# The last batch of a matrix-trace kernel: other load groups, and four rows instead of two on TensorE

## The chip, the cores and the metric

The kernel runs on one core of one Trainium2 chip. The metric is the device time of a run in microseconds (us). The span of the profile is 1.7 to 1.8 us shorter than the time of the same run.

The verdict "faster" or "slower" is given at 2%, which is 14.2 us here.

## The reference

```python
B, N = 8, 2176
prod = np.matmul(a, b)                                           # a, b: [8, 2176, 2176] float32
traces = np.diagonal(prod, axis1=1, axis2=2).sum(axis=-1)        # eight numbers
```

A trace needs no product: it is the sum over i and k of `a[i, k] * b[k, i]`. So the kernel reads both inputs once (303 MB), transposes A on TensorE, and multiplies it with B element by element.

## The kernel before

"Row" means a row block here: 128 rows of B, so a batch has 17 of them, 0 to 16. The loads turn float32 into bfloat16 on the way and are issued from GpSimd. In each batch A is loaded first. TensorE transposes it into PSUM, and ScalarE and VectorE copy it into the tile `at`. Then B is loaded, and VectorE multiplies `at` with B's rows and sums, one instruction for each load group:

```python
def multiply_reduce(x, y, acc, out=None):          # one VectorE instruction, sum into acc
    nc.vector.tensor_tensor_reduce(out=x if out is None else out, in0=x, in1=y, scale=1.0,
                                   scalar=0.0, op0=MUL, op1=ADD, accum_out=acc)
```

In the last batch nothing follows that could hide the work on B. So this batch has smaller load groups, and gives some rows to TensorE. There a row is 17 matmuls of 128 by 128, all added up in one PSUM tile; the diagonal of that tile holds the sums wanted:

```python
    fine = [4, 4, 2, 2, 2, 2, 1]                   # rows in each load of the last batch's B
    PE_ROWS = (13, 15)                             # rows that TensorE takes
    LAST_PIECES = [(0, 2), (2, 3), (3, 5)]         # row 16 is loaded in three pieces
    ...
                (group,), _ = fetch(shared[:, used:used + m, :], b[bi], start, m, 1)
                used += m
                b_t = group[2]
                mine = [s for s in range(m) if v0 + s not in PE_ROWS]
                on_dve(v0 + mine[0], b_t[:, mine[0]:mine[-1] + 1, :])
                for s in range(m):
                    if s not in mine:
                        multiply_on_pe(at, b_t[:, s, :], v0 + s, 0, len(a_groups))
    ...                                            # row 16: TensorE and VectorE share each piece
    for n, (x, y) in enumerate(pe_work):
        nc.tensor.matmul(trace_ps, x, y, start=(n == 0), stop=(n == len(pe_work) - 1))
    ...                                            # VectorE: its share of row 16's pieces, then
    multiply_reduce(tiles[f32], trace_ps, late_acc[:, cols:cols + 1], out=tiles["diagonal"])
    ...                                            # sum over partitions (TensorE, VectorE), store
```

I call the last `multiply_reduce` "the diagonal". It needs TensorE's last matmul, and in program order it follows all of VectorE's other work. About 2.8 us of sums and store come after it.

## Time and profile before

| | kernel before |
|---|---|
| median of six runs | 710.47 us (710.38 to 710.72) |
| span of the profile | 708.7 us |
| HBM read over the span | 428 GB/s |
| busiest compute engine | VectorE, 57% |
| last piece of B landed | 704.30 us |
| VectorE done, diagonal starts | 705.93 us |
| TensorE's last matmul ends | 705.66 us |

The stream of loads fills the span. The tail behind it decides, and it begins with three events that lie within 1.6 us of each other. The groups of VectorE's instructions in the last 37 us of the kernel before say how its work is divided (line, engine, operation, tiles, shapes, count | busy us, mean ns | idle before):

```profile
L133 DVE CUSTOM_DVE_ANT_1 at<-at,shared 128x8704 bf16<-128x8704 bf16 x2 | 18.4, 9223 | 0.5 <-ACT at L128 0.5
L133 DVE CUSTOM_DVE_ANT_1 at<-at,shared 128x4352 bf16<-128x4352 bf16 x2 | 9.3, 4685 | 0.0
L133 DVE CUSTOM_DVE_ANT_1 at<-at,shared 128x2176 bf16<-128x2176 bf16 x2 | 4.8, 2419 | 0.0
```

Six instructions, 32.5 us, with no waiting but 0.5 us at the start: VectorE is behind the loads throughout.

### The profile page before, as it was taken

The numbers are of one execution on the slowest core, as the hardware profiler recorded it, in microseconds if no ns is written. First come the engines' busy times: TensorE is split into PE (matmuls) and PEld (weight loads), VectorE is DVE, ScalarE is ACT, GpSimd is POOL, SyncE is SP. The second block draws the span as 40 slices with busy tenths as digits, with TensorE's granted clock in tenths as the row PEclk, the third lists the DMA queues.
The fourth block names the chain that finished last, engine by engine and source line by source line (L and its number), as shares of the span: only waits on it lengthen the run. The fifth ranks groups of instructions, "written<-read, shape, count | busy, mean of one in ns | idle before, by whom it ended". The sixth has DMA issues, their size and how long they took to land.

```text
span 708.7 us, 3160 instructions
## 1 busy us (share of the span) xinstructions
PE 193.3 (27%) x1271; PEld 179.6 (25%) x1271; DVE 403.7 (57%) x204; ACT 197.2 (28%) x211; POOL 36.0 (5%) x63
## 2 busy tenths in 40 slices
PE   1542006420054100551006600056000670006703
PEld 0542005420054100550006500056000560005602
DVE  0223995138942389423893348933489335883398
ACT  2344005430064200652006510066000670006700
POOL 1000000000010000000001000000000000000100
PEclk9977556765577655776557765577655775557755
DMA  9999999999999999999999999999999999999997
GB/s 220 220 219 214 210 221 220 218 209 214 224 219 214 214 218 221 216 212 216 220 218 216 214 217 220 212 217 218 217 216 215 216 220 218 214 214 217 220 211 145
DMA packets 11681, 152.28 MB, mean 215 GB/s; under 512 B 914, under 2 KB 1170, under 8 KB 3090
## 3 DMA queue, kind: packets, MB, share of 16 engines
q0 software_dynamic: 11520, 150.97, 100.2%
q1 hardware_dynamic: 146, 1.11, 0.5%
q8 instruction: 10, 0.16, 0.1%
q14 instruction: 5, 0.04, 0.0%
HBM read 303.04 MB, written 0.00 MB: 428 GB/s over the span
## 4 chain that ended last, share of the span: by engine, by line
DMA 53%; DVE 27%; another core or an unknown queue 8%; issue 7%; PE 2%; ACT 1%; POOL 0%; DVEq 0%; POOLq 0%
DMA t<-in_b_dram 41%; DVE at L133 27%; DMA t<-in_a_dram 13%; PE ps L167 2%; ACT at L128 1%; POOL t L82 0%; DVE acc L133 0%; PE ps L188 0%; POOL identity masks.py:199 0%; DVE late L133 0%; DVE at L126 0%; DVEq L133 0%; POOL identity masks.py:197 0%; PE total L322 0%
## 5 line engine op out<-in xcount | busy, mean ns | idle before, releaser
L128 ACT COPY at<-ps 128x1024 bf16<-128x1024 bf16 x208 | 194.8, 1045 | 471.6 <-PE ps L167 471.4
L133 DVE CUSTOM_DVE_ANT_1 at<-at,t 128x8704 bf16<-128x8704 bf16 (+1 forms) x35 | 273.6, 7863 | 80.8 <-DMA t<-in_b_dram 80.8
L167 PE MATMUL ps<-identity,t 128*128 128x128 f32 x1088 | 179.3, 332 | 479.2 <-DMA t<-in_a_dram 468.5
L167 PEld LDWEIGHTS ps<-identity,t 128*128 128x128 f32 x1088 | 167.3, 212 | 488.1 <-issue 460.8
L126 DVE COPY at<-ps 128x1024 bf16<-128x1024 bf16 (+2 forms) x104 | 94.1, 907 | 215.4 <-PE ps L167 197.7
L82 POOL DMA_DIRECT2D t<-in_a_dram x23 | 15.4, 669 | 343.2 <-DVE acc L133 199.6
L133 DVE CUSTOM_DVE_ANT_1 at<-at,shared 128x8704 bf16<-128x8704 bf16 (+2 forms) x6 | 32.3, 5442 | 0.5 <-ACT at L128 0.5
L82 POOL DMA_DIRECT2D t<-in_b_dram x23 | 14.8, 646 | 238.8 <-PE ps L188 119.5
L188 PE MATMUL ps<-identity,t 128*128 128x128 bf16 x136 | 14.2, 219 | 5.0 <-DVE at L126 4.6
L188 PEld LDWEIGHTS <-t 128*128 128x128 bf16 x136 | 11.0, 100 | 8.4 <-issue 8.3
L307 PEld LDWEIGHTS <-at 128*128 128x128 bf16 x40 | 4.6, 123 | 28.9 <-issue 28.8
L307 PE MATMUL trace_ps<-shared,at 128*128 128x128 bf16 x32 | 4.0, 293 | 28.4 <-DMA shared<-in_b_dram 28.4
L82 POOL DMA_DIRECT2D shared<-in_b_dram x6 | 3.2, 534 | 55.1 <-PE ps L188 35.8
L101 DVE CAST t<-words 128x1088 bf16<-128x1088 f32 x1 | 0.7, 727 | 5.0 <-DMA words<-in_a_dram 5.0
L133 DVE DVE_READ_ACCUMULATOR2_ANT acc<- 128x1 f32 x35 | 2.9, 83 | 0.0
L100 ACT CAST t<-words 128x1088 bf16<-128x1088 f32 x1 | 1.1, 1099 | 3.8 <-DMA words<-in_a_dram 3.8
L292 POOL DMA_DIRECT2D b_t<-in_b_dram x3 | 1.6, 559 | 0.0
L100 ACT ACT_TABLE_LOAD x1 | 1.3, 1283 | 0.7 <-PEq L346 0.7
L133 DVE CUSTOM_DVE_ANT_1 at<-at,b_t 128x256 bf16<-128x256 bf16 (+1 forms) x3 | 1.4, 507 | 0.0
L265 DVE TENSOR_REDUCE sums<-acc 128x1 f32<-128x5 f32 x7 | 1.1, 157 | 0.2
L307 PE MATMUL trace_ps<-b_t,at 128*128 128x128 bf16 x8 | 1.1, 296 | 0.0
L133 DVE DVE_READ_ACCUMULATOR2_ANT late<- 128x1 f32 x10 | 0.8, 82 | 0.0
(18 smaller groups left out, 4.2 us busy)
## 6 DMA issues: line engine op xcount, KB each, us to landing
t<-in_a_dram POOLq DMA_DIRECT2D x16, 4352.0 KB, 45.5
t<-in_b_dram POOLq DMA_DIRECT2D x14, 4352.0 KB, 51.9
shared<-in_b_dram POOLq DMA_DIRECT2D x2, 2176.0 KB, 42.7
shared<-in_b_dram POOLq DMA_DIRECT2D x4, 1088.0 KB, 34.1
t<-in_a_dram POOLq DMA_DIRECT2D x7, 544.0 KB, 47.4
t<-in_b_dram POOLq DMA_DIRECT2D x6, 544.0 KB, 54.9
words<-in_a_dram SPq DMA_DIRECT2D x1, 1088.0 KB, 5.1
t<-in_b_dram POOLq DMA_DIRECT2D x1, 340.0 KB, 53.7
```

Source lines behind the costliest of these rows:

```text
L82: issued = nc.gpsimd.dma_start(out=part[lo:hi], in_=rows[lo:hi])
L100: nc.scalar.copy(out=t[:, 0, :half], in_=plain[:, :half])
L101: nc.vector.tensor_copy(out=t[:, 0, half:], in_=plain[:, half:])
L126: last_copy = nc.vector.tensor_copy(out=dst, in_=src)
L128: nc.scalar.copy(out=dst, in_=src)
L133: nc.vector.tensor_tensor_reduce(out=x if out is None else out, in0=x, in1=y, scale=1.0, scalar=0.0, op0=MUL, op1=ADD, accum_out=acc,)
L167: nc.tensor.transpose(ps[:, n * m + r, :], words[:, r, c0:c0 + step * (P - 1) + 1:step], tiles[f32],)
L188: last_transpose = nc.tensor.transpose(ps16[:, n, r, :], a_t[:, r, c0:c0 + P], tiles[bf16],)
L265: nc.vector.reduce_sum(out=tiles["sums"][:, bi:bi + 1], in_=acc[:, :cols], axis=mybir.AxisListType.X)
L292: loaded.append(nc.gpsimd.dma_start(out=row[:, lo:hi], in_=b[bi, start:start + P, lo:hi]))
L307: nc.tensor.matmul(trace_ps, x, y, start=(n == 0), stop=(n == len(pe_work) - 1),)
```

## The change

The intent is to take VectorE out of the tail. TensorE, idle most of that time, gets rows 11 and 12 too, and rows 14 and 15 are loaded separately, so that VectorE can have row 14 as soon as it is there.

```diff
-    fine = [4, 4, 2, 2, 2, 2, 1]
+    fine = [4, 4, 4, 2, 1, 1, 1]
-    PE_ROWS = (13, 15)
+    PE_ROWS = (11, 12, 13, 15)
...
-                on_dve(v0 + mine[0], b_t[:, mine[0]:mine[-1] + 1, :])
+                if mine:
+                    on_dve(v0 + mine[0], b_t[:, mine[0]:mine[-1] + 1, :])
```

## The prediction

> **What bounds the kernel now.** I read the page first, then the chain of waits from 590 us on, then the timeline of the last 40 us, then the issues of GpSimd, and last the packets and completion increments of the DMA queue in the trace. The page says that the span is a stream of loads:
>
> ```profile
> span 708.7 us, 3160 instructions
> ...
> DMA  9999999999999999999999999999999999999997
> GB/s 220 220 219 214 210 221 220 218 209 214 224 219 214 214 218 221 216 212 216 220 218 216 214 217 220 212 217 218 217 216 215 216 220 218 214 214 217 220 211 145
> ...
> HBM read 303.04 MB, written 0.00 MB: 428 GB/s over the span
> ```
>
> The DMA engines are at 90% or more in 39 of 40 slices; only the last slice (17.7 us) drops to 7 tenths and 145 GB/s. No compute engine is above 57%. So a change to compute can win only what lies after the last byte, plus stalls of the stream, of which there are none to see. The change touches the last batch alone, so the stage to look at is the last 40 us. The chain of waits there:
>
> ```profile
> 672.42 8.54 DVE at L133
> ...
> 704.35 0.28 issue
> 704.63 0.08 DVE late L133
> 704.71 0.60 DVE at L133
> 705.31 0.01 DVE late L133
> 705.33 0.34 DVE at L133
> ...
> 705.93 0.08 DVE late L133
> 706.01 0.20 DVE diagonal L133
> ```
>
> From 672.42 to 706.21 VectorE is named at nearly every step: it starts when the transposed A is complete, and no gap follows. The "issue" pieces are the inside of long VectorE instructions. The timeline shows the tail of both engines (start, duration, engine, line, instruction):
>
> ```profile
> 690.71 4.68 DVE L133 CUSTOM_DVE_ANT_1 at<-at,shared 128x4352 bf16<-128x4352 bf16 x1
> ...
> 699.94 2.42 DVE L133 CUSTOM_DVE_ANT_1 at<-at,shared 128x2176 bf16<-128x2176 bf16 x1
> 702.28 2.01 PE L307 MATMUL trace_ps<-shared,at 128*128 128x128 bf16 x16 [3.59 <-DMA shared<-in_b_dram]
> ...
> 704.33 1.11 PE L307 MATMUL trace_ps<-b_t,at 128*128 128x128 bf16 x8
> 704.63 0.69 DVE L133 CUSTOM_DVE_ANT_1 at<-at,b_t 128x512 bf16<-128x512 bf16 x1
> ...
> 705.26 0.40 PE L307 MATMUL trace_ps<-at,b_t 128*128 128x128 bf16 x1
> 705.93 0.28 DVE L133 CUSTOM_DVE_ANT_0 diagonal<-identity,trace_ps 128x128 bf16<-128x128 f32 x1
> ```
>
> Two things are to be seen. VectorE is behind: it begins the first of row 16's pieces at 704.63. And TensorE, which waited 3.59 us for rows 14-15 and then ran to 705.66 (705.26 + 0.40), is behind VectorE's end by only 0.27 us (705.93 - 705.66). The completion increments in the trace (sixteen for each load; the last counts) give the landings: rows 8-9 at 686.13, 10-11 at 691.24, 12-13 at 696.42, 14-15 at 702.24, the three pieces of row 16 at 702.89, 703.50 and 704.30. So three things end within 1.6 us of each other: the stream (704.30), TensorE (705.66), VectorE (705.93). After that come the diagonal, the two last sums and the store, 2.81 us (708.74 - 705.93), which the change leaves alone.
>
> **What the Trainium skill says.** (1) "DMA: Bandwidth & Descriptors", section Bandwidth, measures 425 GB/s for a 16 MB load by a single core and derives a ceiling of 435.2 GB/s. The trace agrees: 428 GB/s over the whole span, so the stream has no slack to be won. (2) The same page, "Why a DMA increments its semaphore by 16 and not by 1": only the full 16 means that all data landed, so a load is as late as its slowest engine. The trace agrees: rows 14-15 have fifteen increments by 701.59 and the last at 702.24; a 16,384-byte instruction packet at 700.2 fell among its packets. (3) "VectorE: DVE Perf Modes", the section on the TRN2 errata, gives (N+151)/0.96 ns for an fp32 tensor_tensor add; the page has no row for this custom multiply-and-reduce, but it obeys that formula: 2176 elements give 2424 ns (trace 2419), 4352 give 4691 (4685), 8704 give 9224 (9223). (4) "TensorE: Matmul & The Clock Gate", Part 1: the array runs at half clock until about one window of 3413 ns has been busy. In the trace the grant is 0.50 from 673.99 to the end; it rose to 1.0 elsewhere after windows that I work out as 85% busy or more, and not after windows of up to 76% (a rough count from matmul starts).
>
> **The change, part by part.** *VectorE's work.* Before, rows 0-12 and 14 are its own: fourteen rows in six instructions, 672.42 to 704.63, 32.21 us. Afterwards it has rows 0-3, 4-7, 8-10 and 14: twelve rows in four. The first two take to 690.71 as before. Three rows have 6528 elements: (6528+151)/0.96 = 6.96 us, an estimate by the formula above; row 14 costs 2.42. Sum 18.29 + 6.96 + 2.42 = 27.67, so 4.5 us less. *Where that goes.* Rows 8-11 are one load now and land when 10-11 did, 691.2 to 691.3, so the third instruction starts 0.6 us later and ends at about 698.25. Row 14 has its own load and lands halfway between 696.42 and 702.0, near 699.2; VectorE waits about 1 us and ends it at 701.65. Then it follows row 16's pieces: 702.95 + 0.69 = 703.64; + 0.42 = 704.06; the last lands at 704.30, starts about 704.36 and ends at 704.78. VectorE would be done 1.15 us earlier than the 705.93 of before.
>
> *TensorE's work.* Two more rows, 17 matmuls each. One row costs 2.05 us (702.28 to 704.33). Row 11 runs 691.3 to 693.4, in idle time. Rows 12 and 13 run 696.46 to 700.6, before row 15 is there. So none of the two added rows delays row 15. Row 15 ends with the last byte of the same 2.2 MB (rows 14 and 15) as before and lands at 701.6 if the instruction packet falls elsewhere, 702.24 if it does not. Row 15 and row 16's nine matmuls took 3.38 us (702.28 to 705.66); so TensorE ends between 705.03 and 705.66. It cannot end earlier than about 705.0 anyway: the last piece lands at 704.30, and then three matmuls of its own follow (two at about 0.12 us pitch, and the last one's 0.40).
>
> *The end.* The diagonal then waits for TensorE, no longer for VectorE, and starts about 0.1 us after it (estimate, the hand-over of a semaphore): 705.1 to 705.75, against 705.93. That is 0.2 to 0.8 us won, and I take 0.5.
>
> *Transposes.* Rows 14 and 15 leave the paired fp32 form for single bf16: per group of four A rows, four fp32 transposes fewer and eight bf16 more. At full clock the trace has them 0.11 us and 0.055 us apart, so 0.44 against 0.44 us: nothing. The copies stay 9 for each such group, with the same size; ScalarE sits in a row from 664.04 to 672.42 and sets VectorE's start, so that start stays at 672.4, within 0.3 us. VectorE's later wait swallows such a shift.
>
> *The stream.* Nine loads before and nine after, in the same three buffers, let go by the same instructions. Packets of 17408, 8704 and 4352 bytes take 1302, 662 and 342 ns (medians). Rows 8-11 as one load: 8 packets for each engine, 10.42 us, against 16 x 662 = 10.59; rows 14 and 15 apart: 16 x 342 = 5.47 against 8 x 662 = 5.30. Minus 0.17 and plus 0.17: nothing.
>
> Sum: 710.49 - 0.5 = **710.0 us**.
>
> **The rivals.** *The whole VectorE saving arrives* (4.5 us, 706.0). For it: the chain of waits is VectorE throughout. Against it: the last byte lands at 704.30 and VectorE's end was 705.93, so no compute change can win more than 1.6 us. I give this nothing. *TensorE takes VectorE's place with no gain*: if row 15 lands at 702.24 again, or later because single-row packets end less evenly over the engines, the gain shrinks to 0.2 us or nothing, 710.3 to 710.5. For it: the 0.27 us between the two engines. *The stream gets longer*: another mean rate of small packets at the end, where the three pieces of row 16 already have packets of 1024 to 2048 bytes, or an issue that comes later because a transposition ends later. Queued loads stand 25 us ahead (rows 12-13 issued at 670.68, landed at 696.42), which speaks against the second. It would make 710.7 to 711. *The clock comes up*: rows 12 and 13 fill the window from 697.88 to 701.29 to about 77%, on the edge of what raised the grant elsewhere. Row 15 would then be quick, and the end would be set by the last landing: 709.6 to 709.8.
>
> **Range and chances.** Most weight lies between the second rival and the fourth, 709.6 to 710.5. The three runs of before differ by 0.34 us, which I add around it: 709.2 to 710.8. Two per cent are 14.2 us; there is nothing in these parts that moves a tenth of that in either direction. So within 2%: 0.98, and 0.01 on each side.
>
> **What would show each step right or wrong.** Right: VectorE has idle time before row 14's instruction, released by the load of row 14, and again before row 16's pieces; the 3-row instruction lasts about 6.95 us; the diagonal is released by TensorE rather than following VectorE; the last piece lands at 704.3 within 0.3; VectorE starts at 672.4. Wrong: VectorE without gaps to the end; the last landing beyond 704.8; row 15's matmuls starting later than 702.4; a grant of 1.0 after 701 (then the gain is nearer 0.8). A time above 711 would mean that the stream, not the tail, was hurt, and below 709 that it got shorter, which I see no reason for.

## The result, and the profile after

The changed kernel took 709.68 us (median of six runs, 709.64 to 710.19), the kernel before 710.47: 0.79 us less. Ratios are computed as the mean time of one kernel's runs over that of the other's of the same rounds, so they are not quite the ratio of the medians. Here the ratio is 0.999, with an interval from 0.9977 to 1.0003. The slowest of the six runs lies below the fastest of the other six.

The page of the changed kernel has the same stream:

```profile
span 707.9 us, 3257 instructions
...
DMA  9999999999999999999999999999999999999997
...
HBM read 303.04 MB, written 0.00 MB: 428 GB/s over the span
```

What differs is the end of the chain of waits (start, us, what):

```profile
671.22 30.32 DMA shared<-in_b_dram
701.54 0.04 issue
701.58 3.39 PE trace_ps L308 x26
...
705.12 0.29 DVE diagonal L133
```

Where VectorE stood from 672 us on, the chain now has one load (row 15, landed at 701.54) and then TensorE's 26 matmuls for rows 15 and 16. The timeline of the same stretch shows VectorE waiting, which it did not do there before:

```profile
691.32 6.96 DVE L133 CUSTOM_DVE_ANT_1 at<-at,shared 128x6528 bf16<-128x6528 bf16 x1 [1.10 <-DMA shared<-in_b_dram]
...
699.05 2.42 DVE L133 CUSTOM_DVE_ANT_1 at<-at,shared 128x2176 bf16<-128x2176 bf16 x1 [0.77 <-DMA shared<-in_b_dram]
...
701.58 2.01 PE L308 MATMUL trace_ps<-shared,at 128*128 128x128 bf16 x16 [0.91 <-DMA shared<-in_b_dram]
702.82 0.69 DVE L133 CUSTOM_DVE_ANT_1 at<-at,b_t 128x512 bf16<-128x512 bf16 x1 [1.34 <-DMA b_t<-in_b_dram]
...
704.26 0.43 DVE L133 CUSTOM_DVE_ANT_1 at<-at,b_t 128x256 bf16<-128x256 bf16 x1 [0.36 <-DMA b_t<-in_b_dram]
704.56 0.40 PE L308 MATMUL trace_ps<-at,b_t 128*128 128x128 bf16 x1
705.12 0.29 DVE L133 CUSTOM_DVE_ANT_0 diagonal<-identity,trace_ps 128x128 bf16<-128x128 f32 x1 [0.42 <-PE trace_ps L308]
```

VectorE waits for a load before four of its last five multiplications, in the square brackets. It ends row 16 at 704.69, and the diagonal waits 0.42 us more for TensorE. TensorE starts row 15 at 701.58, not 702.28 as before, and ends 0.70 us earlier, at 704.96.

So the 0.81 us (705.93 to 705.12) have two parts. The last piece landed 0.06 us earlier (704.24 against 704.30). And the diagonal starts 0.88 us after that landing, no longer 1.63. The second part, 0.75 us, is what the experiments are about. There is something odd in it: row 15 is the end of the same bytes as before, and yet it was complete 0.70 us earlier (702.24 before, 701.54 after). A 16,384-byte packet of instructions passed at 700.2 in the kernel before; in the changed kernel the last such packet passed at 673.0. So there are two candidates: the work that was moved away from VectorE, and a packet that happened to move.

### The profile page after: what moved, and what is told of

It reads as the page before. It is cut to its first block, busy times and chain, and to the rows that moved or that the text cites. A ratio compares the mean times of both kernels' runs of the same rounds, so it can differ in the third digit from the quotient of the medians.

```text
span 707.9 us, 3257 instructions
## 1 busy us (share of the span) xinstructions
PE 194.4 (27%) x1322; PEld 180.3 (25%) x1322; DVE 399.6 (56%) x200; ACT 196.5 (28%) x211; POOL 36.0 (5%) x63
## 4 chain that ended last, share of the span: by engine, by line
DMA 58%; DVE 24%; another core or an unknown queue 8%; issue 6%; PE 2%; ACT 1%; POOL 1%; DVEq 0%; POOLq 0%
DMA t<-in_b_dram 41%; DVE at L133 23%; DMA t<-in_a_dram 13%; DMA shared<-in_b_dram 4%; PE ps L167 1%; ACT at L128 1%; DVE at L126 1%; PE trace_ps L308 0%; POOL t L82 0%; PE ps L188 0%; POOL shared L82 0%; DVE acc L133 0%; POOL identity masks.py:199 0%; DVEq L133 0%
## 5 line engine op out<-in xcount | busy, mean ns | idle before, releaser
L167 PE MATMUL ps<-identity,t 128*128 128x128 f32 x1071 | 174.2, 328 | 481.8 <-DMA t<-in_a_dram 471.1
L167 PEld LDWEIGHTS ps<-identity,t 128*128 128x128 f32 x1071 | 162.0, 213 | 491.1 <-issue 463.0
L133 DVE CUSTOM_DVE_ANT_1 at<-at,shared 128x8704 bf16<-128x8704 bf16 (+2 forms) x4 | 27.8, 6955 | 1.9 <-DMA shared<-in_b_dram 1.9
L188 PE MATMUL ps<-identity,t 128*128 128x128 bf16 x170 | 16.4, 219 | 5.1 <-DVE at L126 4.7
L188 PEld LDWEIGHTS <-t 128*128 128x128 bf16 x170 | 13.0, 100 | 8.5 <-issue 8.2
L308 PEld LDWEIGHTS <-at 128*128 128x128 bf16 x72 | 8.3, 124 | 24.7 <-issue 24.5
L308 PE MATMUL trace_ps<-shared,at 128*128 128x128 bf16 x64 | 8.1, 294 | 23.9 <-DMA shared<-in_b_dram 23.9
L308 PE MATMUL trace_ps<-at,shared 128*128 128x128 bf16 x4 | 1.6, 396 | 0.0
```

The lines of the kernel that those rows point to most:

```text
L167: nc.tensor.transpose(ps[:, n * m + r, :], words[:, r, c0:c0 + step * (P - 1) + 1:step], tiles[f32],)
L188: last_transpose = nc.tensor.transpose(ps16[:, n, r, :], a_t[:, r, c0:c0 + P], tiles[bf16],)
```

## The experiments

A word on reading them. On the chips of the experiments the times of one kernel move by up to 1.4 us from run to run (the kernel before: 710.29 to 711.72 in the three sets of nine), more than what is sought. The trace offers a steadier measure: the time from the last landing of B to the start of the diagonal, called **the lag** here. It leaves out when the stream ended. It is from one profile for each kernel. In the experiments with no unused matmuls or only 17, the profiled run was the fastest of its five; the others took 0.6 to 1.3 us longer, and what their traces would show is not known. The edits are shown against the changed kernel, that of fetch_before against the kernel before.

| kernel | last landing | diagonal starts | lag | last to be ready | median (before beside it) | ratio of means |
|---|---|---|---|---|---|---|
| before | 704.30 | 705.93 | 1.63 | VectorE | 710.47 | |
| changed | 704.24 | 705.12 | 0.88 | TensorE | 709.68 (710.47) | 0.9990 |
| groups_only | 704.29 | 706.51 | 2.22 | VectorE | 711.89 (711.15) | 1.0010 |
| pe_rows_only | 704.30 | 705.27 | 0.97 | VectorE | 710.64 (711.15) | 0.9995 |
| fetch_before | 704.33 | 705.45 | 1.12 | VectorE | 710.85 (711.15) | 0.9995 |
| fetch_after | 705.45 | 706.84 | 1.39 | TensorE | 711.07 (711.15) | 0.9997 |
| after_again | 704.32 | 705.20 | 0.88 | TensorE | 710.70 (711.09) | 0.9995 |
| three_rows | 704.38 | 705.25 | 0.87 | TensorE | 710.64 (711.09) | 0.9991 |
| pair_kept | 704.26 | 705.23 | 0.97 | VectorE | 710.77 (711.09) | 0.9993 |
| fetch_after_2 | 705.22 | 706.71 | 1.49 | TensorE | 711.15 (711.09) | 0.9999 |
| fetch_control | 705.37 | 706.26 | 0.89 | TensorE | 710.79 (711.17) | 0.9993 |

All of them give correct results. The interval of every ratio has 1 in it, so what is concluded below rests on the lags and the traces and not on these times. The run after_again is the changed kernel, unaltered, on the chip of three_rows, pair_kept and fetch_after_2. Its lag was 0.88 us again, released by TensorE, as expected; the time was expected 0.7 to 0.9 us below the kernel before, and the medians lie only 0.39 us apart. The size of the gain in time, 0.79 us in the first comparison, was not found again.

### The groups alone: groups_only

```diff
-    PE_ROWS = (11, 12, 13, 15)
+    PE_ROWS = (13, 15)
```

> The new groups (4, 4, 4, 2, 1, 1, 1) with the old rows 13 and 15 on TensorE. My theory (the gain needs VectorE out of the way, and the groups alone don't do that): rows 8-11 are one instruction of 8704 elements that can't start before its load lands at 691.3, where VectorE used to have rows 8-9 from 690.7 on; it frees VectorE at 700.5, then rows 12 and 14 (2.34 us each) take it to 705.1 and row 16's three pieces to 706.4. The diagonal starts at 706.4 with VectorE last, 0.5 us later than before: 711.0 us, 0.5 above before and 1.3 above the changed kernel. Rival (the gain is an earlier landing of row 15, for which the single-row loads are enough): row 15 lands at 701.5, and the time is near 709.7 to 710.

Row 15 landed at 701.58, as the rival wanted it. It did not help. The timeline:

```profile
691.36 9.22 DVE L133 CUSTOM_DVE_ANT_1 at<-at,shared 128x8704 bf16<-128x8704 bf16 x1 [1.10 <-DMA shared<-in_b_dram]
...
705.21 0.68 DVE L133 CUSTOM_DVE_ANT_1 at<-at,b_t 128x512 bf16<-128x512 bf16 x1
```

VectorE waits 1.10 us for the group of four, is then without a gap, and takes up row 16 at 705.21, 0.9 us after its last piece landed. The lag grows to 2.22 us. The groups alone make the end later, and the rival falls.

### The TensorE rows alone: pe_rows_only, and one pair kept: pair_kept

```diff
-    fine = [4, 4, 4, 2, 1, 1, 1]
+    fine = [4, 4, 2, 2, 2, 2, 1]      # pe_rows_only
+    fine = [4, 4, 4, 2, 2, 1]         # pair_kept: rows 14 and 15 in one load
```

> The old groups (4, 4, 2, 2, 2, 2, 1) with four rows on TensorE. My theory: VectorE has rows 8-9 and 10 done by 697.6 and then waits for row 14, which now comes only with row 15, at 701.5; it ends row 14 at 704.0 and the three pieces at about 705.5, while TensorE is done at 705.0. VectorE is last by 0.5 us, the diagonal starts at about 705.5: 710.1 us, between the two. Rival (taking rows off VectorE is all there is to it, the groups do nothing): 709.7 as in the changed kernel. A landing of rows 14-15 at 702.2 instead would make it 710.7.

> The changed kernel with rows 14 and 15 in one load as before (groups 4, 4, 4, 2, 2, 1). My theory: of the new groups only the separate load of row 14 matters; here VectorE waits idle from 698.2 to 701.6 for row 14, ends it at 704.0 and the pieces at 705.3, as in the run with the old groups and four rows on TensorE (diagonal 0.97 us after the last landing): 0.1 to 0.4 us slower than the changed kernel, VectorE last. Rival (the group of four, rows 8-11, is what gives or costs time): the same as the changed kernel.

In the timeline of the kernel with the rows alone, VectorE waits long for row 14 and then has no more gaps:

```profile
701.62 2.43 DVE L133 CUSTOM_DVE_ANT_1 at<-at,shared 128x2176 bf16<-128x2176 bf16 x1 [4.13 <-DMA shared<-in_b_dram]
...
705.27 0.28 DVE L133 CUSTOM_DVE_ANT_0 diagonal<-identity,trace_ps 128x128 bf16<-128x128 f32 x1
```

With the pair kept the same line is

```profile
701.57 2.43 DVE L133 CUSTOM_DVE_ANT_1 at<-at,shared 128x2176 bf16<-128x2176 bf16 x1 [3.24 <-DMA shared<-in_b_dram]
```

and both lags are 0.97 us. So with the four rows on TensorE nearly all of the gain in the lag is there (0.66 of 0.75 us), and of the new groups only the separate load of row 14 counts, for 0.09 us (0.97 - 0.88). The group of four gives nothing. But the instruction packet had moved in both runs too: it fell at 694.9 and 694.8, in the load of rows 12 and 13, and rows 14 and 15 landed at 701.60 and 701.55. So these two runs do not separate the rows from the packet; the last experiments do. I had expected 705.5 for the diagonal of the kernel with the rows alone; it was 705.27, because VectorE's last three instructions follow each other faster (0.61, 0.35 and 0.34 us from start to start) than their durations of 0.69, 0.42 and 0.42 say. Both theories' times were too close together for the rounds to separate (710.64 and 710.77, beside 710.70 for the changed kernel on the chip of the second).

### One row fewer on TensorE: three_rows

```diff
-    PE_ROWS = (11, 12, 13, 15)
+    PE_ROWS = (12, 13, 15)
```

> The changed kernel with row 11 back on VectorE (rows 12, 13, 15 on TensorE). VectorE's third instruction has 8704 elements again, 691.3 to 700.5, row 14 follows without a gap to 702.8, and row 16's first piece (landed 702.8) starts there. My theory (TensorE and the landings set the end of the changed kernel, so VectorE's 0.8 and 1.3 us of waiting are free to be filled): the same time as the changed kernel within 0.1 us, the diagonal still released by TensorE. Rival (each row taken off VectorE shortens the end by some of its 2.3 us): 0.3 us or more slower than the changed kernel.

The lag is 0.87 us, and TensorE releases the diagonal. VectorE's work fills its waiting time: the third instruction lasts 9.23 us again and ends near 700.7, and row 14 follows at once:

```profile
700.62 2.42 DVE L133 CUSTOM_DVE_ANT_1 at<-at,shared 128x2176 bf16<-128x2176 bf16 x1
...
705.25 0.29 DVE L133 CUSTOM_DVE_ANT_0 diagonal<-identity,trace_ps 128x128 bf16<-128x128 f32 x1 [0.42 <-PE trace_ps L308]
```

Row 11 on TensorE is worth nothing; three rows are enough. This run also started VectorE's chain at 672.43, as late as the kernel before, without any harm.

### Moving the instruction packet: fetch_before, fetch_after, fetch_control

The Trainium skill ("Runtime: NRT & Kernel Launch", section Instruction fetch mechanics) says that an engine's instructions are refilled in blocks of 16 KiB, 256 instructions, over DMA. If the packets are TensorE's, unused matmuls in idle time (a weight load and a matmul each, two instructions) move them:

```diff
+        if bi == 1:                                  # after batch 1's transposes
+            spare = psum_small.tile([P, P], f32, tag="spare")
+            with tc.issue_after(last_transpose.ins):
+                for _ in range(17):                  # 94 and 128 in the changed kernel
+                    nc.tensor.matmul(spare, tiles[bf16], tiles[bf16], start=True, stop=True)
```

> The kernel before, with 17 unused matmuls on TensorE after batch 1's transposes, in its idle time, so that TensorE's instruction count at the end of the last transposes is that of the changed kernel. My theory: the 16,384-byte instruction packet is fetched for TensorE's stream, every 256 instructions; it moves from 700.2 to about 673, and rows 14-15 land at 701.55 instead of 702.24, so that TensorE ends at 705.0 instead of 705.66. But VectorE still ends at 705.93, so the time stays: 710.4 to 710.5. Rival (the earlier landing alone makes the gain): 709.8. If the packet doesn't move, the packet is not TensorE's.

The packet moved from 700.2 to 673.1 with 34 instructions more, and rows 14-15 landed at 701.62. TensorE took row 15 at 701.67 and ended at 705.06, but VectorE had no gap and came last:

```profile
701.80 2.42 DVE L133 CUSTOM_DVE_ANT_1 at<-at,shared 128x2176 bf16<-128x2176 bf16 x1
...
705.45 0.28 DVE L133 CUSTOM_DVE_ANT_0 diagonal<-identity,trace_ps 128x128 bf16<-128x128 f32 x1
```

The expectation failed in one point: the diagonal started 0.48 us earlier than in the kernel before, although I had expected no gain. The earlier landing is not the cause. VectorE started its chain at 671.79 instead of 672.42, 0.63 us earlier, and needed as long as before (33.66 us to the diagonal; 33.51 before). The transposes were quicker, because the clock grant rose to 1.0 at 662.25 and not at 663.75: between these times the transposes are 0.11 us apart in this run and 0.21 us in the kernel before. I come back to that below.

> The changed kernel, with 94 unused matmuls in the same place, so that the next fetch (256 instructions on) falls after row 12's matmuls, at about 700.2 as in the kernel before. My theory: one engine of the sixteen loses about 0.6 us, row 15 lands at 702.1 to 702.2, TensorE starts it then and ends at 705.6, and the diagonal with all after it comes 0.6 us later: 710.3 us, leaving 0.2 of the gain of 0.8. Rival (the packet has nothing to do with it): 709.7.

> The same kernel as fetch_after, whose rounds fell on a chip with landings that moved by up to 1 us between runs; now beside the changed kernel. The instruction packet falls at 700 to 701 again, row 15's last increment comes about 0.5 us after the fifteenth, and the diagonal starts about 1.4 us after the last piece of row 16 instead of 0.88: 0.4 to 0.6 us slower than the changed kernel. If the packet costs nothing: the same.

With 94 matmuls the packet fell at 701.2 and 701.0 in the two profiles. One increment of row 15's load came 0.52 and 0.63 us after the fifteenth, TensorE began row 15 that much later, and the lags are 1.39 and 1.49 us. The chain of waits of the first:

```profile
703.26 0.04 issue
703.30 3.39 PE trace_ps L314 x26
...
706.84 0.29 DVE diagonal L133
```

Both runs had one thing more, which I had not foreseen: all of the stream's end was late, the last piece at 705.45 and 705.22 instead of 704.3. So I needed a control in which the matmuls are there and the packet is not.

> The changed kernel with 128 unused matmuls instead of 94, so 256 instructions more than without any: a whole fetch more, and the following fetches at the same places as in the changed kernel (the last near 673 us). It is the control for the two runs with 94. My theory (what counts is where the packet falls): no packet in the tail, row 15's last increment within 0.1 us of the fifteenth, and the diagonal 0.85 to 0.95 us after the last landing, as in the changed kernel, not 1.4 to 1.5 as with 94. Rival (the unused matmuls themselves disturb the end): 1.2 us or more after the last landing again. The time below the kernel before by 0.3 to 0.8, unless an engine lags as in the runs with 94.

With 128 matmuls, exactly 256 instructions, one more packet was fetched in the whole run, and the last one fell at 674.1, as without them. The last landing was late again (705.37). Row 15's last increment came 0.40 us after its fifteenth, more than the 0.1 I had expected, but as far as in the loads before and after it (0.38 to 0.39 us from 682 us on), so it is late together with the whole stream and not set apart. TensorE releases the diagonal 0.89 us after the last landing:

```profile
702.72 3.40 PE trace_ps L314 x26
...
706.26 0.29 DVE diagonal L133
```

So the unused matmuls do not lengthen the lag; the packet inside row 15's load does, by 0.5 to 0.6 us. The late stream, on the other hand, is there in the profiles of all three runs with 94 or 128 matmuls. That the matmuls cause it is not shown: the four runs of after_again, the changed kernel itself, whose traces were not read took 710.46 to 710.98 us, those of the control, on another chip, 710.52 to 710.96. In the time of the rounds the packet shows as 711.15 against 710.70 for the changed kernel on the same chip, 0.45 us; the late stream is in that difference too, so this number is not a clean measure of the packet.

What is left after the landing is TensorE's 26 matmuls and VectorE's last piece, which end 0.27 us apart (704.96 and 704.69), so a shift of work between them can win only a part of that; three_rows is as good as the changed kernel and has less on TensorE.

## Why the prediction was right or wrong

The time, 709.68, lies in the range, and the mechanism was the predicted one: VectorE leaves the chain, TensorE and the last landings take its place. Point by point:

- **VectorE's work.** Right. The predicted 6.96 us for three rows were 6.96, and the four instructions have 27.8 us busy for a predicted 27.67. Row 14's load landed at 698.93, not 699.2, and VectorE was done at 704.69, not 704.78. Most of the 4.5 us saved became waiting: 1.10 + 0.77 + 1.34 + 0.36 = 3.57 us stand in the brackets above, and 0.42 before the diagonal.
- **TensorE's work.** Right. The two added rows ran before row 15 was there. TensorE ended at 704.96, just before the early end of "between 705.03 and 705.66", because the packet did fall elsewhere. The hand-over to the diagonal took 0.16 us (704.96 to 705.12), for an estimate of 0.1, for which the prediction named no source.
- **The size.** The forecast of 0.5 was the middle of two cases, 0.2 with the packet and 0.8 without; it was the second. The prediction left the packet's place open as a matter of chance, so that the better case came was luck on its part. The runs show that the place is none: it follows from TensorE's instruction count. In all eleven profiles the last packet starts 1.7 to 3.1 us after TensorE's matmuls and weight loads in the trace reach 2487 in number, or 2743, which is 256 more, in the three runs with 94 or 128 unused matmuls. The load that is under way then is the one it meets. The change has 34 more instructions by the end of the last transposes (17 more transposes, two instructions each), and the same 34, put into the kernel before, moved the packet to the same place. The profile of before had the times of all packets, so this could have been looked for in advance.
- **How the 0.75 us divide.** With the packet in row 15's load the changed kernel has lags of 1.39 and 1.49 us, so moving the work alone gives 0.14 to 0.24 us of the 1.63. With the packet gone but VectorE last, an earlier row 15 gives nothing; this is read from the trace of fetch_before, where VectorE has no gap and its earlier start (0.63 us) accounts for the shorter lag (0.51 us). Both together give 0.75. So some 0.5 to 0.6 us of the gain come from a by-product of the change, which VectorE's relief made visible.
- **"That start stays at 672.4, within 0.3 us."** Wrong: it was 671.70. The prediction looked for the cause in the transposes and found none, which was right: three_rows has the same transposes as the changed kernel and starts at 672.43. What it left out is the phase of the clock grant. In the profiles without a late stream the start follows when the grant rose to 1.0: 660.6 to 662.3 gives 671.70 to 671.79 (changed, after_again, groups_only, pair_kept, fetch_before), and 663.2 to 663.8 gives 672.15 to 672.43 (before, three_rows, pe_rows_only). The change does not set it: the changed kernel and three_rows are the same program up to there, with rises at 661.17 and 663.69. As predicted, VectorE's waiting swallowed the shift in the changed kernel; in the kernel before it would have counted in full, as fetch_before shows.
- **The stream and the groups.** Right that they cost nothing: the last landing was 704.24. The worry about single-row packets was not borne out.
- **The rival "the clock comes up".** Its step "row 15 would then be quick" is wrong. In pe_rows_only the grant did rise to 1.0, at 700.78, before row 15. The stretches of one row each, at a grant of 0.50 and of 1.00 (stretch, us, busy of TensorE and of its weight loads, grant, DMA share, GB/s):

```profile
696.99:699.04 2.05, 2.05 (x17) 1.96 (x17) 0.50 1.03 217
701.64:703.69 2.05, 2.05 (x18) 1.94 (x18) 1.00 0.93 161
```

  A row costs 2.05 us at either grant. Nor does the prediction's edge between 76% and 85% hold in the later traces. By the time that matmuls fill of a window (an estimate from the traces), the grant rose in pair_kept at 699.85 after 86%, and in three_rows it stayed at 0.50 after windows of 88% and 86%.

## What to carry to other kernels

Where a stream fills the span, work out first what lies behind the last landing; that bounds what any shift of work can win, here 1.6 of 4.5 us. When several engines end close together, relieving one wins only the distance to the next, so list each engine's end and what holds it, and look for the smallest relief that suffices (here three rows, not four). And before crediting a change of tenths of a microsecond to its intent, check whether it has moved something that follows the instruction count, such as an instruction packet in the last load.

## What the Trainium skill lacked or had wrong

- "TensorE: Matmul & The Clock Gate" gives a spacing of 107 ns for N = 128 at half clock and 56 ns when warm, and about 81 ns for a sustained stream of weight loads and matmuls. The 94 unused matmuls on contiguous operands, each with its weight load, took 0.056 us at a grant of 1.0. The rows' matmuls took about 0.116 us from start to start at 0.50 and at 1.00 alike. They read the moving operand (the one streamed through the array, not the loaded weights) in steps of four bf16 elements; that this is the reason was not tested.
- "Runtime: NRT & Kernel Launch", section Instruction fetch mechanics, calls the cost of crossing a block boundary mostly hidden. The refill in steps of 256 TensorE instructions agrees with the runs. It was not hidden for the load whose packets it met: in five profiles with a packet inside one of the last loads (before, pe_rows_only, pair_kept, fetch_after, fetch_after_2) that load's last increment came 0.65, 0.52, 0.47, 0.52 and 0.63 us after its fifteenth.
- "DMA: Bandwidth & Descriptors" has no figure for how far the sixteen engines drift apart in a long stream. In the kernel before, the first and the sixteenth increment of a load are 0.44 us apart at the start and 2.1 at the end, and in the control 3.2. In the kernel before the step from 0.6 to 1.6 us comes with the load after an instruction packet at 51.8. In the control the steps from 2.2 to 2.9 and from 2.9 to 3.3 come after the packets at 645.4 and 674.1. But most packets are followed by no such step (in the kernel before, none after those at 126 to 378 us). That packets cause the drift, and with it the late stream of the three runs and perhaps the scatter of the times, was not tested.
- "VectorE: DVE Perf Modes" has no row for the multiply-and-reduce used here. The page's formula for an fp32 tensor_tensor fits it with bf16 operands: 6.96 us predicted and measured for 6528 elements.
